# Four of seven low-part subtractions moved from POOL to DVE through a PSUM bank, weight rows of a new set requested closer together, and every fourth row's low part moved to POOL

## The chip, the core and the metric

The kernel runs on one core of one Trainium2 chip. The metric is the device time of one execution, in microseconds (us). Five engines work side by side, each on its own instruction stream, in the order in which the program gives the instructions to it: PE (TensorE, matrix products), DVE (VectorE), ACT (ScalarE), POOL (GpSimd) and SP (SyncE, which here issues nearly all DMA transfers). An instruction that waits for another engine holds up everything behind it on its own engine. A second view of PE, PEld, is the loading of weights, which overlaps the products.

## What is computed

One encoder block on x of 1024 tokens by 2048: a root-mean-square norm, one input projection, two head groups (windowed attention with a relative bias, and retention run in both directions), a norm and a gate for each branch, one output projection with a residual, and a final norm. The part that matters here is the end:

```python
mixed = jnp.concatenate([attn.astype(x.dtype), ret], axis=-1)
x = x + jnp.einsum('bse,ed->bsd', mixed, w_out[l])
return rmsnorm(x, final_norm_w)
```

Here `mixed` is 1024 by 2048 and `w_out` 2048 by 2048, both float32.

## The kernel before

**High and low parts.** PE multiplies in a rounded 32-bit format (`F32R`). To keep float32 accuracy each operand is split into a high part (the value rounded, written by ACT) and a low part (the value minus its high part). A product is then three matmuls: high by high, high by low, low by high. These are lines 1167, 1168 and 1169 in `multiply`. The stationary operand is `wh` (high) and `wl` (low); the moving one is a row, a tile `h` of 128 by 1024 whose first half is the high part and whose second half is the low part.

**Seven products.** Half of the input projection (the first pass of the loop over `slots`) and the whole output projection (the loop over `oslots`, line 1596) use a scheme with seven products, p = 0 to 6, in place of eight. In the output projection the stationary side comes from `mixed` (tile `xm`, four quarters `raws[q, 0..3]` and their combinations `sums[q]`), the moving side from combinations of `w_out`, precomputed earlier in the kernel and stored in `wc`. A tile q has seven slots, one for each p, and a slot is 12 matmuls of 512 columns: four blocks j by three. There are 16 output tiles, numbered o = q - NF from 0 to 15, so 112 slots. In `slot_list` (line 1230) the tiles interleave: (q,0), (q,1), (q-1,6), (q,2), (q-1,5), (q,3), (q,4). In the text slots of the output projection are numbered from 0, in that order.

**Rows and sets.** Four tiles o share one set of 28 rows (seven p by four j): set st = o // 4. `place` (line 1155) gives the row's buffer: it is the same for every set, `(16, 20, 0, 4, 8, 24, 12)[p] + j`, so its number modulo 4 is j. A new row therefore can't be loaded before the last matmul of the old one. After slot (q, p) of the last tile of a set (`o % 4 == 3`, line 1613) `o_rows` puts the four rows of that p for the next set into the list `todo`, from two points later on. The rows of the first set are put there while the input projection's last units run (line 1546). Stretches in which rows are replaced are called set changes: they begin in slots 19, 47 and 75, and the first slots that need the new rows are 26, 54 and 82.

**Points.** `point()` is called once per four-matmul-block step, that is once for each j: four points to a slot. Each point calls `rows_tick` (line 1045). It takes at most one row off `todo`, issues its load on SP (`row_load`), and moves the time of the next one on by `rgap` points. Ten points later the row's high part follows on ACT (`row_high`), and two points after that the low part (`row_low`, line 1040), on DVE, in place. `rows_done` (line 1061) is called ahead of a slot and forces whatever of its rows has not been given out yet. By counting points through lines 1045 to 1069 one gets the slot in which each of these instructions stands in the program. With `rgap` 2.0 the four rows of (next set, p = 4), needed in slot 32, have their loads in slots 28.25 to 29.75 and their low parts in 31.25, 31.75, 32 and 32, the last two forced by `rows_done`.

**Preparing the stationary side.** In slot n, at j = 1, `between` calls `prep` (line 1148) for slot n + 2: ACT writes `wh`, then POOL writes `wl` as source minus `wh` (`split`, line 171, with engine `G`). There are three buffers of each. `prep_sums` (line 1135) makes the combinations on POOL: four operations a tile. `raw_load` fetches the quarters on SP. So POOL does seven low parts and four combinations for each tile.

**Collecting.** After each slot DVE adds the PSUM bank to a tile (`o_collect`, line 1457). Banks are used again by later products of the same tile: slot p = 4 adds on top of the bank that p = 2 left, so its first matmul has to wait for that collect. In the last two sets ACT then squares the sums, writing the unused squares to a PSUM bank (line 1474), and in the last set `finish` (line 1480) norms a block: a short chain of small DVE operations with one POOL power in it, and four larger DVE products.

**Other work in the stretch.** The retention of the last head pairs runs through the first 18 or so slots of the output projection, with its own matmuls, its transposes into the three PSUM buffers of tag `ST` (`pS`, `pT`, lines 153 to 157), and scans on DVE.

Of the kernel before, what the change touches and what calls it, by code (L numbers as in the profile page):

```python
# [9 lines left out]
F32 = mybir.dt.float32  # L10
F32R = mybir.dt.float32r
AF = mybir.ActivationFunctionType
ALU = mybir.AluOpType
# [20 lines left out]
NS, NF = len(STD), len(FAST)  # L34
# [5 lines left out]
def hybrid_block(ctx: ExitStack, tc: tile.TileContext, a: dict, out: bass.AP):  # L40
    nc = tc.nc
    ctx.enter_context(tc.manual_schedule(engines={mybir.EngineType.Pool}))
    V, A, G, T, SP = nc.vector, nc.scalar, nc.gpsimd, nc.tensor, nc.sync
# [40 lines left out]
    def new_row(r, dt=F32R):  # L84
        rows[r] = hp.tile([128, 1024], dt, tag=f"h{r}", name=nm(f"h{r}_"), bufs=1)
        return rows[r]
# [38 lines left out]
    def flush(everything=False):  # L125
        while pend and (everything or pend[0][0] <= pt[0]):
            pend.popleft()[1]()
# [10 lines left out]
    def wpair(i):  # L138
        return w_high(), w_low()
# [10 lines left out]
    def psum(tag, bufs):  # L150
        return ps.tile([128, 512], F32, tag=tag, name=nm("ps" + tag), bufs=bufs)

    def pS():
        return psum("ST", 3)
# [7 lines left out]
    def pM():  # L162
        return [psum("Ma", 2), psum("Ma", 2), psum("Mb", 2), psum("Mb", 2)]

    def tt(eng, o, x, y, op):
        eng.tensor_tensor(o, x, y, op)  # L166
# [4 lines left out]
    def split(o_hi, o_lo, x, eng=None):  # L171
        A.copy(o_hi, x)  # L172
        tt(eng or V, o_lo, x, o_hi.bitcast(F32), ALU.subtract)
# [93 lines left out]
    def drain(queue, until):  # L267
        while until not in done:
            if not queue:
                flush(True)  # L270
                if until is None or until in done:
                    return
            g, _ = queue[0]
            try:
                queue[0] = (g, next(g))
            except StopIteration:
                queue.popleft()
# [645 lines left out]
    def spare(n):  # L923
        return rows[16 + n // 2][:, 512 * (n % 2) : 512 * (n % 2) + 512]
# [49 lines left out]
    def w_combine():  # L974
        plan = []

        def load(st, j, x, n):
            SP.dma_start(x[n], w_row(st, n // 2, n % 2, j))

        def less(x, n, m):  # L980
            tt(G, x[m], x[n], x[m], ALU.subtract)

        def less_to(x, n, m):
            tt(G, x[n], x[n], x[m], ALU.subtract)

        def keep(st, p, j, x):
            SP.dma_start(wc[st, 4 * p + j], x)

        for g in range(16):
            st, j = divmod(g, 4)  # L990
            x = [spare(4 * (g % 3) + n) for n in range(4)]
            t = 25 * g
            for n in range(4):
                plan.append((t + 4 * n, load, st, j, x, n))

            plan += [
                (t + 26, less, x, 1, 0), (t + 30, less, x, 3, 1),
                (t + 34, less_to, x, 3, 0), (t + 38, less_to, x, 2, 3),
                (t + 35, keep, st, 3, j, x[0]), (t + 39, keep, st, 4, j, x[1]),
                (t + 43, keep, st, 2, j, x[3]), (t + 47, keep, st, 5, j, x[2]),  # L1000
            ]
        yield from planned(plan)
        done.add("wc")
# [27 lines left out]
    todo, parts, rgap, rnext = deque(), deque(), [2.4], [0]  # L1031
# [7 lines left out]

    def row_low(key, r, src):  # L1040
        hi, lo = rows[r][:, 0:512], rows[r][:, 512:1024]
        tt(V, lo, lo.bitcast(F32), hi.bitcast(F32), ALU.subtract)
        done.add(key)

    def rows_tick():
# [102 lines left out]
    def prep(q, p):  # L1148
        src = {0: 0, 1: 1, 3: 2, 4: 0, 5: 3}.get(p)
        src = sums[q] if src is None else raws[q, src]  # L1150
        hi, lo = wpair(q)
        split(hi, lo, src, G)
        ready_w[q, p] = (hi, lo)

    def place(q, p, j):
# [32 lines left out]
    def quarter(b):  # L1188
        return et_(("e11", "e12", "e2", "e2")[b])
# [99 lines left out]
    for u, (kind, i) in enumerate(STD):  # L1289
# [5 lines left out]
        for pos in range(NK):  # L1295
# [35 lines left out]
            for b in range(4):  # L1331
                p = plain[b]
# [28 lines left out]
    def retention(p):  # L1361
        yield ready(("qk", p), ("vr", p), "ret")
        if p == 3:
            pace[0] = 1.9
        yield from ret_job(p)
# [23 lines left out]
    for n, (q, p) in enumerate(slots):  # L1389
# [3 lines left out]
        def between():  # L1393
            if n + 2 < len(slots):
                prep(*slots[n + 2])
            run_later()
# [19 lines left out]
    def o_rows(at, st, p):  # L1416
        for j in range(4):
            todo.append((at, ("row", st, p, j), place(NF, p, j), wc[st, 4 * p + j]))
# [101 lines left out]
    for u, (kind, i) in enumerate(FAST):  # L1520
        if u == 4:
            drain(jobs, ("attn", 3))
            drain(aux, ("sum", 3))
            drain(jobs, "attn_norm")
            flush(True)
            ph_ctx.close()
            phase[0] = ph_ctx.enter_context(tc.tile_pool(name="ret", bufs=1, reuse_waits="tile"))
            done.add("ret")
            pace[0], apace[0] = 3.0, 2.2
            e = mybir.EngineType  # L1530
            ctx.enter_context(tc.manual_schedule(engines={e.PE, e.DVE, e.Activation, e.SP}))
            for g in range(4):
                jobs.append((retention(g), None))
            for hf in range(2):
                SP.dma_start(spare(22 + hf), rbd[:, 512 * hf : 512 * hf + 512])
        if u == 0:
            for r in range(16, 28):
                new_row(r, F32)
            for hf in range(2):
                SP.dma_start(spare(12 + hf), a["cos"][:, 512 * hf : 512 * hf + 512])  # L1540
                SP.dma_start(spare(14 + hf), a["sin"][:, 512 * hf : 512 * hf + 512])
            side.append((w_combine(), None))
        whole = pM()
        if u == 13:
            rgap[0] = 3.3
            for p, at in ((0, 20), (1, 40), (2, 73), (3, 81), (4, 89), (6, 97), (5, 105)):
                o_rows(pt[0] + at, 0, p)
        elif u == NF - 1:
            rgap[0] = 2.0
        if u == 0:  # L1550
            whole = [whole[0], whole[2], whole[3], whole[1]]
        tiles = []
        for w in range(4):
            wi = W_STD + 4 * u + w
            step[0] = 16 * NS + 8 * u + 2 * w
            w_load(wi + 3)
            wh, wl = wsp.pop(wi)
            if u == 0:
                rows_done([("x", r) for r in range(4 * w, 4 * w + 4)])
            for b in range(4):  # L1560
                et, hf = b // 2, b % 2
                p = whole[b]
                if kind == "ga" and (w, b) == (2, 0):
                    attention_rows(i)
                if w == 1 + b // 2:
                    tiles.append(quarter(b))
                    SP.dma_start(tiles[b], yd[u, b])
                for kk in range(2):
                    ws = slice(256 * kk + 128 * et, 256 * kk + 128 * et + 128)
                    row = 2 * (2 * w + kk) + hf  # L1570
                    hh, hl = rows[row][:, 0:512], rows[row][:, 512:1024]
                    last = (w, kk) == (3, 1)
                    T.matmul(p, wh[:, ws], hh, start=(w, kk) == (0, 0), stop=False)  # L1573
                    T.matmul(p, wh[:, ws], hl, start=False, stop=False)  # L1574
                    T.matmul(p, wl[:, ws], hh, start=False, stop=last)  # L1575
                    if last:
                        tt(V, tiles[b], p, tiles[b], ALU.add)
                    point()
                if u == NF - 1:
                    first_slots(w, b)  # L1580
                if b == 0 and wi == W_STD:
                    w_split(wi + 1)
                if b == 1:
                    w_split(wi + 2)
        if kind == "ga":
            gates.append((attention_gates(i, tiles), None))
        elif kind == "gr":
            post.append((gate_post(kind, i, tiles), None))
        elif kind == "qk":
            post.append((rope_post(i, tiles), None))  # L1590
        else:
            post.append((value_post(i, tiles), None))
# [3 lines left out]
    for n, (q, p) in enumerate(oslots):  # L1596
        slot[0] = n
        o = q - NF
        st = o // 4
        prepare(q, p, NF)  # L1600
        for x in wanted.pop(n, ()):
            o_request(*x)

        def between():
            if n + 2 < len(oslots):
                o_ready(n + 2)
                prep(*oslots[n + 2])
            run_later()

        rows_done([("row", st, p, j) for j in range(4)])  # L1610
        multiply(q, p, between)
        o_collect(q, p)
        if o % 4 == 3 and st < 3:
            rgap[0] = 2.0
            o_rows(pt[0] + 2, st + 1, p)
    run_later(True)
    drain(aux, None)
# [104 lines left out]
```

## Time and profile before

| what | value |
|---|---|
| device time, median of 3 runs | 1531.51 us (1528.52 to 1531.87) |
| device time of the profiled execution | 1533.07 us |
| span of the profiled execution, first to last instruction | 1531.3 us |
| mean granted PE clock | 0.994 |
| output projection, first to last matmul | 1156.2 to 1516.7 us |

The page counts an engine as busy while an instruction of it runs. On PE the matmuls overlap: one is shown as 0.39 us long, while the next starts about 0.23 us after it. A small stall of PE therefore shows as idle time only where it is longer than this overlap, and the time lost is better read from how many matmuls a stretch of given length holds. In the groups a line such as L166 is that of a helper (`tt`), so groups are told apart by tiles: `wl<-r,wh` is a low part of the stationary side, `h<-h` a row's low part, `r<-r,r` a combination, `e<-psMa,e` a collect.

### The profile page before, as it was taken

How to read it: one execution, taken by the hardware profiler on the slowest of the kernel's cores; microseconds unless marked ns; L12 is line 12 of the kernel's file. 1: busy time of each engine (PE TensorE's matmuls, PEld its weight loads, DVE VectorE, ACT ScalarE, POOL GpSimd, SP SyncE). 2: the span in 40 equal slices, each digit the busy share in tenths (PEclk: the TensorE clock that was granted, in tenths of full speed). 3: DMA queues.
4: the chain of work that ended last, by engine and by line, in shares of the span. 5: the costliest groups of instructions: out<-in, count | busy, mean ns of one | idle time of the engine just before them, and what ended most of it. 6: DMA issues, size and time to landing. Idle time of an engine off the chain costs nothing.

```text
span 1531.3 us, 22172 instructions
## 1 busy us (share of the span) xinstructions
PE 1463.1 (96%) x7250; PEld 1218.4 (80%) x7250; DVE 922.0 (60%) x1791; ACT 660.4 (43%) x1401; POOL 844.6 (55%) x641
## 2 busy tenths in 40 slices
PE   8999998999999999999999999999999998989985
PEld 6998886777888888888788888788887776868764
DVE  5573333864565565565424755754869868483986
ACT  5311133775676675776221232132244243354522
POOL 3232221245546655655666656566446677687863
PEclk9999999999999999999999999999999999999998
DMA  8879889986456456446888589497496586765654
GB/s 304 287 259 337 283 264 314 283 277 203 123 168 162 135 168 186 128 153 208 308 283 268 172 278 355 164 313 271 149 305 240 157 297 217 269 241 182 206 166 144
DMA packets 225072, 353.18 MB, mean 231 GB/s; under 512 B 31883, under 2 KB 86155, under 8 KB 223548
## 3 DMA queue, kind: packets, MB, share of 16 engines
q1 hardware_dynamic: 194492, 330.78, 65.5%
q10 hardware_dynamic: 30464, 20.98, 4.4%
q8 instruction: 57, 0.93, 0.2%
q14 instruction: 59, 0.48, 0.1%
HBM read 239.97 MB, written 124.29 MB: 238 GB/s over the span
## 4 chain that ended last, share of the span: by engine, by line
PE 71%; DMA 9%; DVE 7%; issue 6%; POOL 4%; ACT 2%; SPq 1%; ACTq 0%; DVEq 0%; POOLq 0%
PE psMa L1168 5%; PE psMa L1167 5%; PE psMa L1169 5%; PE psMb L1169 4%; PE psMa L1573 4%; PE psMb L1573 4%; PE psMb L1168 4%; PE psMb L1167 4%; PE psMb L1575 4%; PE psMb L1574 4%; PE psMa L1575 4%; PE psMa L1574 4%; DVE h L166 2%; DMA h<-wc 2%; PE psST L605 2%
## 5 line engine op out<-in xcount | busy, mean ns | idle before, releaser
L166 POOL TENSOR_TENSOR wl<-r,wh 128x512 fp32r<-128x512 f32 x288 | 393.2, 1369 | 400.7 <-ACT wh L172 380.1
L172 ACT CAST wh<-r 128x512 fp32r<-128x512 f32 x288 | 177.5, 619 | 304.2 <-PE psMa L1168 70.8
L1168 PE MATMUL psMa<-h,wh 128*128 128x512 f32 x512 | 201.9, 394 | 7.4 <-DVE h L166 7.2
L1167 PE MATMUL psMa<-h,wh 128*128 128x512 f32 x512 | 203.0, 397 | 4.2 <-DVE t L166 3.5
L1169 PE MATMUL psMa<-h,wl 128*128 128x512 f32 x512 | 200.9, 392 | 0.0
L166 DVE TENSOR_TENSOR h<-h 128x512 fp32r<-128x512 f32 x156 | 174.3, 1146 | 22.9 <-ACT h L1038 22.9
L166 POOL TENSOR_TENSOR r<-r,r 128x512 f32<-128x512 f32 x128 | 182.1, 1423 | 2.8
L166 POOL TENSOR_TENSOR wl<-e,wh 128x512 fp32r<-128x512 f32 x48 | 73.0, 1523 | 199.0 <-ACT wh L172 194.9
L1169 PE MATMUL psMb<-h,wl 128*128 128x512 f32 x384 | 151.4, 394 | 7.9 <-POOL wl L166 7.8
L1167 PE MATMUL psMb<-h,wh 128*128 128x512 f32 x384 | 151.9, 396 | 3.0 <-ACT e L1201 1.7
L1168 PE MATMUL psMb<-h,wh 128*128 128x512 f32 x384 | 150.8, 393 | 2.4 <-DVE h L166 2.3
L166 DVE TENSOR_TENSOR e<-psMa,e 128x512 f32<-128x512 f32 x86 | 58.8, 685 | 106.5 <-PE psMa L1575 79.5
L1168 PEld LDWEIGHTS psMa<-h,wh 128*128 128x128 f32 x512 | 96.6, 189 | 29.4 <-DVE h L166 12.8
L1167 PEld LDWEIGHTS psMa<-h,wh 128*128 128x128 f32 x512 | 96.5, 188 | 23.1 <-issue 3.7
L1169 PEld LDWEIGHTS psMa<-h,wl 128*128 128x128 f32 x512 | 96.5, 189 | 21.0 <-POOL wl L166 0.6
L1573 PE MATMUL psMa<-h,wh 128*128 128x512 f32 x256 | 104.0, 406 | 2.5 <-DVE e L166 2.5
L1573 PE MATMUL psMb<-h,wh 128*128 128x512 f32 x256 | 103.4, 404 | 0.0
L1575 PE MATMUL psMa<-h,wl 128*128 128x512 f32 x256 | 100.0, 391 | 0.0
L1038 ACT CAST h<-h 128x512 fp32r<-128x512 f32 x156 | 90.4, 616 | 22.4 <-DMA h<-cd 9.7
L1575 PE MATMUL psMb<-h,wl 128*128 128x512 f32 x256 | 100.0, 390 | 0.0
L1574 PE MATMUL psMa<-h,wh 128*128 128x512 f32 x256 | 99.8, 390 | 0.0
L1574 PE MATMUL psMb<-h,wh 128*128 128x512 f32 x256 | 99.8, 390 | 0.0
(268 smaller groups left out, 3282.8 us busy)
## 6 DMA issues: line engine op xcount, KB each, us to landing
h<-wc SPq DMA_DIRECT2D x112, 256.0 KB, 5.1
r<-in_w_fast SPq DMA_DIRECT2D x64, 256.0 KB, 3.1
r<-in_w_half SPq DMA_DIRECT2D x64, 256.0 KB, 4.7
h<-in_w_out SPq DMA_DIRECT2D x64, 256.0 KB, 5.0
e<-yd SPq DMA_DIRECT2D x64, 256.0 KB, 4.7
wc<-h SPq DMA_DIRECT2D x64, 256.0 KB, 4.5
r<-xm SPq DMA_DIRECT2D x64, 256.0 KB, 4.1
t<-in_xT SPq DMA_DIRECT2D x31, 512.0 KB, 5.9
```

The lines of the kernel that those rows point to most:

```text
L166: eng.tensor_tensor(o, x, y, op)
L172: A.copy(o_hi, x)
L605: T.transpose(p[:, c0], x[:, c0], ident)
L1038: A.copy(rows[r][:, 0:512], rows[r][:, 512:1024].bitcast(F32))
L1167: T.matmul(bank, wh[:, ws], hh, start=(j == 0 and p in (0, 1, 3)), stop=False, skip_group_check=True)
L1168: T.matmul(bank, wh[:, ws], hl, start=False, stop=False, skip_group_check=True)
L1169: T.matmul(bank, wl[:, ws], hh, start=False, stop=(j == 3), skip_group_check=True)
L1573: T.matmul(p, wh[:, ws], hh, start=(w, kk) == (0, 0), stop=False)
L1574: T.matmul(p, wh[:, ws], hl, start=False, stop=False)
L1575: T.matmul(p, wl[:, ws], hh, start=False, stop=last)
```

## The change

Four edits, all in the lines named above. `row_low` does the low part of the rows of the output projection on POOL where the buffer's number is 3 modulo 4 (j = 3, one row in four), and on DVE otherwise. `prep` treats the output projection's products p = 0, 4, 5 and 6 differently: after the high part ACT writes a second copy of it into a PSUM buffer of tag `ST`, and DVE, not POOL, subtracts that copy from the source. Products 1, 2 and 3 stay as they were. And `rgap` is 1.4 in place of 2.0 from the last unit of the input projection on, and at each set change.

```diff
     def row_low(key, r, src):
         hi, lo = rows[r][:, 0:512], rows[r][:, 512:1024]
-        tt(V, lo, lo.bitcast(F32), hi.bitcast(F32), ALU.subtract)
+        tt(G if key[0] == "row" and r % 4 == 3 else V, lo, lo.bitcast(F32), hi.bitcast(F32), ALU.subtract)
         done.add(key)
...
         hi, lo = wpair(q)
-        split(hi, lo, src, G)
+        if q >= NF and p in (0, 4, 5, 6):
+
+            c = pS()
+            A.copy(hi, src)
+            A.copy(c.bitcast(F32R), src)
+            tt(V, lo, src, c, ALU.subtract)
+        else:
+            split(hi, lo, src, G)
         ready_w[q, p] = (hi, lo)
...
         elif u == NF - 1:
-            rgap[0] = 2.0
+            rgap[0] = 1.4
...
         if o % 4 == 3 and st < 3:
-            rgap[0] = 2.0
+            rgap[0] = 1.4
             o_rows(pt[0] + 2, st + 1, p)
```

## The prediction

> **What bounds the kernel now.** I read the page's engine shares first, then the waits of PE over the output projection (1156 to 1517 us), then a table of stretches, and last the groups of one set change.
>
> ```profile
> PE 1463.1 (96%) x7250; PEld 1218.4 (80%) x7250; DVE 922.0 (60%) x1791; ACT 660.4 (43%) x1401; POOL 844.6 (55%) x641
> ```
>
> PE is busy for 96% of the span, so little can be won except where PE stalls. The edits touch only the output projection, so only its stalls count.
>
> ```profile
> engine line waited for: us in total, times, longest us
> PE psMa L1168 <- DVE h L166: 7.2, 10, 0.7
> PE psMb L1169 <- POOL wl L166: 6.6, 5, 1.6
> PE psMa L1167 <- DVE t L166: 3.5, 3, 2.0
> PE psO L812 <- DVE ST L169: 3.2, 1, 3.2
> ```
>
> In order: the low part of a new row comes late from DVE; `wl` comes late from POOL; a bank's collect comes late from DVE; a retention scan comes late. These figures are idle time behind overlapping matmuls and understate the loss. Stretches of equal length show it whole:
>
> ```profile
> core 0: us, PE busy (x) PEld busy (x) DVE busy (x) ACT busy (x) POOL busy (x), PEclk, DMA share, GB/s
> 1256.00:1280.00 24.00, 19.73 (x79) 13.69 (x78) 23.18 (x21) 10.53 (x20) 20.28 (x13) 1.00 0.86 294
> 1290.00:1314.00 24.00, 24.00 (x108) 19.87 (x106) 8.00 (x13) 5.61 (x9) 16.87 (x14) 1.00 0.62 183
> 1339.00:1363.00 24.00, 19.76 (x81) 14.47 (x80) 23.18 (x22) 13.37 (x26) 22.96 (x15) 1.00 0.90 321
> 1364.00:1408.00 44.00, 44.00 (x196) 36.44 (x195) 18.18 (x25) 18.75 (x40) 33.01 (x25) 1.00 0.38 128
> 1420.00:1444.00 24.00, 21.12 (x87) 15.40 (x86) 23.18 (x24) 14.69 (x32) 18.90 (x13) 1.00 0.71 242
> 1456.00:1500.00 44.00, 36.85 (x154) 27.97 (x153) 34.58 (x53) 13.16 (x29) 30.98 (x26) 1.00 0.53 168
> 1156.00:1180.00 24.00, 20.80 (x111) 17.53 (x110) 23.17 (x42) 11.09 (x22) 12.46 (x12) 0.94 0.73 262
> 1180.00:1204.00 24.00, 24.00 (x132) 20.11 (x131) 21.65 (x48) 7.59 (x15) 17.05 (x12) 0.99 0.37 113
> ```
>
> A quiet 24 us holds 108 matmuls, 0.222 us each. The three set changes hold 79, 81 and 87, so they lose 29 x 0.222 = 6.4, 27 x 0.222 = 6.0 and 21 x 0.222 = 4.7 us: **17.1 us in all**. The last stretch holds 154 where a quiet 44 us holds 196: 42 x 44 / 196 = **9.4 us**. In the set changes DVE is busy 23.18 of 24 us, and in the quiet rows a third of the time. A slot takes 12 x 0.222 = 2.7 us.
>
> Why DVE is full in a set change is in its groups, here from 1245 to 1279, with POOL's beside them, and POOL's in a quiet stretch (1284 to 1322) last:
>
> ```profile
> L166 DVE TENSOR_TENSOR h<-h 128x512 fp32r<-128x512 f32 x20 | 27.7, 1421 | 0.0
> L166 DVE TENSOR_TENSOR e<-psMa,e 128x512 f32<-128x512 f32 x6 | 4.1, 680 | 2.0 <-DMA h<-wc 2.0
> L166 DVE TENSOR_TENSOR e<-psMb,e 128x512 f32<-128x512 f32 x4 | 2.7, 678 | 0.0
> ...
> L166 POOL TENSOR_TENSOR wl<-r,wh 128x512 fp32r<-128x512 f32 x10 | 15.9, 1596 | 5.6 <-ACT wh L172 5.6
> L166 POOL TENSOR_TENSOR r<-r,r 128x512 f32<-128x512 f32 x7 | 11.9, 1704 | 0.2
> ...
> L166 POOL TENSOR_TENSOR wl<-r,wh 128x512 fp32r<-128x512 f32 x15 | 20.0, 1336 | 10.2 <-ACT wh L172 10.2
> ```
>
> Three rows from DVE's order of time, the first where POOL did not overlap, the others of one operation on one value per partition:
>
> ```profile
> 1151.20 0.69 DVE L166 TENSOR_TENSOR h<-h 128x512 fp32r<-128x512 f32 x1
> ...
> 1479.48 1.24 DVE L166 TENSOR_TENSOR ft<-fv,fy 128x1 f32<-128x1 f32 x1 [1.39 <-POOL fy L166]
> 1480.76 0.16 DVE L166 TENSOR_TENSOR ft<-ft,fy 128x1 f32<-128x1 f32 x1
> ```
>
> A row's low part takes 0.69 us alone and 1.42 in the set change; POOL's subtraction takes 1.34 and 1.60. The collect, which reads one operand from PSUM, keeps its 0.68. So DVE with two SBUF operands and POOL take turns, and DVE with a PSUM operand does not. Adding turns up for the 34 us: 17 POOL operations x 1.34 + 20 rows x 0.69 = 22.8 + 13.8 = 36.6 us, about the whole stretch. Adding up DVE alone: 27.7 + 4.1 + 2.7 = 34.5. Both are full; PE waits for what they can't do.
>
> The Trainium skill, page "SBUF — State Buffer", section "SBUF: two separate sides", describes such a lock: DVE with two SBUF inputs and GpSimd share one port pair, and whichever starts first keeps it for its whole instruction. The trace agrees (1.24 against 0.16 us for the same small operation). By it, a low part read from PSUM is free of the lock; without it the sum below would keep the price of 1.42 a row, its lower bound.
>
> **The change part by part.** *Low parts of p = 0, 4, 5, 6.* Of the ten `wl` subtractions in that stretch, six leave POOL: 6 x 1.34 = 8.0 us of its turns. Each becomes a DVE subtraction with a PSUM operand; nearest row, the collect: 6 x 0.68 = 4.1 us on DVE, without a turn. ACT gets a second copy for each. ACT writing PSUM is shown by the squares, SBUF to SBUF by the high parts:
>
> ```profile
> L172 ACT CAST wh<-r 128x512 fp32r<-128x512 f32 x75 | 46.2, 620 | 89.3 <-PE psMa L1168 33.8 <-PE psMb L1168 16.8 <-DMA r<-xm 16.4
> L1038 ACT CAST h<-h 128x512 fp32r<-128x512 f32 x58 | 32.7, 615 | 0.0
> L1474 ACT ACTIVATE psO<-y 128x512 f32<-128x512 f32 x16 | 9.6, 603 | 13.5 <-DVE y L166 13.5
> ```
>
> I take 0.62 us: 16 tiles x 4 = 64 copies, 39.7 us spread over 360, hidden by ACT's idle time (10.5 to 14.7 of 24 us busy in the set changes). If that cover is gone, the high parts of rows queued behind come up to 0.62 later each. The new waits: DVE waits for ACT's copy, and the collects and rows behind it wait too. ACT can write only when slot n - 1 has freed `wh`, and DVE then has that slot's collect to do (0.68) and a row, against two ACT operations (1.24). So I cost the wait at nothing, at most 0.6 a slot where no row stands between.
>
> *Rows on POOL.* Up to the last row of p = 4, five of 20 rows leave DVE. DVE: 15 x 1.42 + 10 x 0.68 + 4.1 = 32.2 us against 34.5, if a row stays as dear: 2.3 us won. By turns: (17 - 6 + 5) x 1.34 + 15 x 0.69 = 21.4 + 10.4 = 31.8 against 36.6: **4.8 us won**. If rows fell to 0.69 DVE would need 21.3 and nothing would be late. I take the turns, since they explain the 34 us of before; the ends are 2.3 a change (6.9 in all) and the whole stall (17.1).
>
> The Trainium skill, page "GPSIMD Engine Reference", section "8. Key points", speaks against this edit: elementwise work is about twice as fast on DVE. The rows agree (1.34 against 0.69), and by them the five rows add 5 x 0.65 = 3.3 us of turns; alone they would lengthen the change to 39.9, and it is the six low parts that pay for it.
>
> *Requests at 1.4.* With 2.0 points a row, p = 4's low parts stand in the program in slots 31.25 to 32, its deadline being slot 32. With 1.4 I count 29.75 to 30.75; those of p = 3 move from 29.25-30.75 to 28.5-29.5 (due 31), those of p = 2 from 27.25-28.75 to 26.5-27.5 (due 29). That gives DVE and ACT at least one slot of slack where they had none, and without it freed time on DVE could not be used: the work stood too late in its queue. The loads go on SP's queue ahead of other loads:
>
> ```profile
> h<-wc SPq DMA_DIRECT2D x112, 256.0 KB, 5.1
> ...
> 1263.23 0.38 SPq L1035 DMA_DIRECT2D h<-wc  x1
> ...
> 1243.00:1259.00 16.00, 15.97 (x71) 12.94 (x70) 13.97 (x14) 8.78 (x17) 11.46 (x8) 1.00 1.04 367
> 1323.00:1340.00 17.00, 17.00 (x76) 14.08 (x76) 12.08 (x14) 8.16 (x16) 9.29 (x8) 1.00 1.02 385
> ```
>
> The last row of p = 4 went out at 1263.2 and took some 5 us, and DVE's rows waited for nothing (idle 0.0 in their group): loads were not what was late. But the DMA engines are full (367 to 385 GB/s) in the first third of a change, so earlier requests partly only queue. What is late next are the quarters `r<-xm` behind them; I give back 0.7 us a change for this.
>
> Set changes: 4.8 + 4.8 + 4.7 (no more was lost) - 3 x 0.7 = **12.2 us**.
>
> *Start.* From 1156 to 1204 DVE is busy 44.8 of 48 us with retention and rows. It gets about ten low parts (6.8 us), loses the j = 3 rows and some turns, and the copies now share the `ST` buffers with the retention. I take 0, between -3 (the 3.2 us wait for a scan, doubled) and +3 (gone).
>
> *End.* Counted by matmuls, three of the five late `wl` are of p = 6, two of them in the last stretch; they stood on POOL behind combinations, and now don't. Against it, DVE is behind there:
>
> ```profile
> 1463.70 0.39 PE L1167 MATMUL psMa<-h,wh 128*128 128x512 f32 x1
> ...
> 1471.82 0.68 DVE L166 TENSOR_TENSOR e<-psMa,e 128x512 f32<-128x512 f32 x1
> ```
>
> PE leaves slot 95 at 1463.7, and DVE collects it at 1471.8, 8.1 us later. A low part for slot n + 2 stands behind the collect of slot n - 1, so it comes in time only while that lag is below two slots, 5.4 us. With fewer rows left over and fewer turns I expect a smaller lag: a gain of 2 us, between +6 and -6.
>
> **Sum.** 12.2 + 0 + 2 = 14.2 us off. The profiled execution took 1533.07 us, 1.56 over the median of 1531.51: 1518.9 there, **1517.3 against the median**. Bounds: 6.9 - 3 - 6 = -2.1 and 17.1 + 3 + 6 = 26.1 us.
>
> **The rivals.** *Requests outrun the DMA engines.* At 367 to 385 GB/s nothing lands sooner; only the slack of program order and part of the turns are won. For: these two rates. Against: DVE's rows waited for no load. About 5 us won: 1526.5. *The stall moves.* Rows j = 3 stand on POOL behind combinations that wait for `r<-xm`; PE then waits for POOL's row in place of DVE's, and the sum is nothing: 1531. For: POOL is busy 18.9 to 23.0 of 24 us in the changes. Against: six operations leave for five that come, on the cheaper side. *DVE's lag decides (slower).* Where DVE is more than 5.4 us behind, each moved low part makes PE wait, and that stall delays the next. At the start and in the last stretch some ten moved low parts stand behind such lags; a loss of 1.5 us for six of them is 9, and if DVE's waits for ACT (0.6 a slot) eat the 4.8 us, nothing is won in the changes: 1531.5 + 9 = 1540.5. For: the 8.1 us. Against: a lag in a change is bounded by the work that now leaves.
>
> **Chances.** Forecast 0.65 (1510 to 1523), DMA 0.17, moved stall 0.08, DVE's lag 0.10. A measurement here can tell about 0.2%, 3 us. Faster by more than that: 0.65 + 0.17 = 0.82; same 0.08; slower 0.10. The range reaches from most of the upper bound (1508) to the DMA rival's upper side (1529); the slower case and the moved stall stay outside.
>
> **What would show it.** Right: the three 24 us stretches of a change hold some 100 matmuls or more; `h<-h` on DVE drops from 1.42 towards 1.0 us; the new subtraction takes about 0.68 whatever POOL does; waits of line 1168 for DVE's rows all but vanish. Wrong: a line 1169 waiting for DVE's `wl` by over a microsecond, a line 1168 waiting for POOL's `h`, ACT's `wh` waiting longer for `r<-xm`, or retention matmuls waiting for an `ST` buffer.

## The result, and the profile after

The changed kernel took **1518.1 us** (median of 4 runs, 1517.59 to 1521.51) against 1531.36 us for the kernel before beside it (4 runs, 1528.52 to 1531.87). The ratio is 0.9922, with a 95% interval of 0.9903 to 0.9941. The profiled execution took 1517.67 us with a span of 1515.9 us, 15.4 us less than the one of before; by the medians 13.3 us came off. In the new file the three matmul lines of `multiply` are L1174, L1175 and L1176, ACT's copy into PSUM is L1156, and `wh` of the four moved products is L1155.

Engine shares of the change, from the page:

```profile
PE 1461.7 (96%) x7250; PEld 1220.7 (81%) x7250; DVE 911.5 (60%) x1827; ACT 689.6 (45%) x1465; POOL 790.5 (52%) x605
```

The 64 moved low parts stand on DVE, whose busy time nevertheless fell by 10.5 us. POOL lost 54 us and ACT gained 29. So other work on DVE became cheaper; the groups further down show which.

What PE waited for in the change, 1156 to 1517 us (line, engine it waited for, total us, times, longest):

```profile
engine line waited for: us in total, times, longest us
PE psO L812 <- DVE ST L169: 3.1, 1, 3.1
PE psMb L1176 <- POOL wl L166: 1.9, 3, 0.7
PE psMa L1176 <- DVE wl L166: 1.9, 3, 0.9
PE psMb L1176 <- DVE wl L166: 1.0, 3, 0.4
...
PE psMb L1174 <- ACT wh L172: 0.2, 1, 0.2
...
PE psMa L1175 <- DVE h L166: 0.2, 1, 0.2
```

DVE's rows held PE for 9.5 us before (7.2 in the group that the prediction shows, 2.3 in the `psMb` one) and hold it for 0.2 now. POOL's `wl` fell from 6.6 to 1.9 in its main group, with 0.5 in another. The new wait is for DVE's own `wl`, 2.9 us in six pieces under a microsecond; five of them stand in or just behind a set change, in slots 32, 35, 37, 63 and 88. The retention's scan (L812) is where it was, and ACT's high parts, behind which the copies now stand, held PE for 0.2 us.

Stretches of the change, moved earlier so that each meets about the same slots as its counterpart of before (the columns are those of the prediction's table):

```profile
core 0: us, PE busy (x) PEld busy (x) DVE busy (x) ACT busy (x) POOL busy (x), PEclk, DMA share, GB/s
1253.00:1277.00 24.00, 22.91 (x99) 17.94 (x98) 23.04 (x25) 16.92 (x33) 21.32 (x15) 1.00 0.93 316
...
1333.00:1357.00 24.00, 22.60 (x98) 17.70 (x97) 20.69 (x24) 16.71 (x32) 19.78 (x14) 1.00 0.95 343
...
1412.00:1436.00 24.00, 23.02 (x99) 17.89 (x97) 21.11 (x26) 18.51 (x39) 17.37 (x13) 1.00 0.79 267
1440.00:1484.00 44.00, 41.55 (x177) 32.40 (x177) 38.48 (x67) 19.94 (x44) 26.39 (x22) 1.00 0.50 163
```

The set changes hold 99, 98 and 99 matmuls where they held 79, 81 and 87; 108 is a quiet stretch. What is lost behind these windows they don't show. The last stretch holds 177 where it held 154. DVE is still busy 20.7 to 23.0 of 24 us in the changes: it was relieved, not emptied.

The same by whole slots, for the kernels that the experiments use. The loss of a stretch is the distance between the first matmuls of the slots at its two ends, less 2.72 us for each slot between. The last column is the start of the output projection, which differs by 1 to 3 us between executions of one kernel (the change 1156.4 and 1159.1). Each row is one execution, and the kernel before has only one.

| us lost in | slots 19-39 | 47-67 | 75-95 | 96-111 | starts at |
|---|---|---|---|---|---|
| before | 6.6 | 6.0 | 7.0 | 9.4 | 1156.2 |
| **the change** | 3.6 | 3.1 | 3.0 | 4.6 | 1156.4 |
| the change again | 2.6 | 4.3 | 3.0 | 4.7 | 1159.1 |
| requests alone | 3.7 | 5.7 | 4.9 | 8.2 | 1154.1 |
| PSUM low parts alone | 2.0 | 5.2 | 3.3 | 6.7 | 1157.2 |
| rows on POOL alone | 6.6 | 8.1 | 10.2 | 6.8 | 1159.5 |
| requests and PSUM | 2.2 | 3.6 | 0.0 | 4.4 | 1155.3 |
| the same again | 1.5 | 4.5 | 0.0 | 4.6 | 1156.6 |
| PSUM and rows, requests at 2.0 | 1.5 | 2.5 | 1.8 | 6.6 | 1156.6 |

In the retention's part (slots 0 to 18) the change took 77.5 us against 78.4.

### The profile page after: what moved, and what is told of

Its sections match the earlier page's. It is cut to its first block, busy times and chain, and to the rows that moved or that the text cites. A ratio compares the mean times of both kernels' runs of the same rounds, so it can differ in the third digit from the quotient of the medians.

```text
span 1515.9 us, 22190 instructions
## 1 busy us (share of the span) xinstructions
PE 1461.7 (96%) x7250; PEld 1220.7 (81%) x7250; DVE 911.5 (60%) x1827; ACT 689.6 (45%) x1465; POOL 790.5 (52%) x605
## 4 chain that ended last, share of the span: by engine, by line
PE 73%; DVE 8%; DMA 6%; issue 4%; POOL 4%; ACT 3%; SPq 1%; DVEq 0%; ACTq 0%; POOLq 0%
PE psMa L1174 5%; PE psMa L1176 5%; PE psMa L1175 5%; PE psMb L1176 4%; PE psMb L1174 4%; PE psMb L1175 4%; PE psMa L1580 4%; PE psMb L1580 4%; PE psMb L1581 4%; PE psMa L1582 4%; PE psMb L1582 4%; PE psMa L1581 4%; PE psST L605 2%; DVE h L166 2%; PE psST L1353 1%
## 5 line engine op out<-in xcount | busy, mean ns | idle before, releaser
L166 POOL TENSOR_TENSOR wl<-r,wh 128x512 fp32r<-128x512 f32 x224 | 300.7, 1344 | 403.2 <-ACT wh L172 373.9
L172 ACT CAST wh<-r 128x512 fp32r<-128x512 f32 x224 | 138.4, 619 | 231.2 <-PE psMb L1581 71.2
L1174 PE MATMUL psMa<-h,wh 128*128 128x512 f32 x512 | 202.9, 396 | 2.3 <-DVE y L166 0.8
L1176 PE MATMUL psMa<-h,wl 128*128 128x512 f32 x512 | 200.9, 392 | 2.6 <-DVE wl L166 1.9
L1175 PE MATMUL psMa<-h,wh 128*128 128x512 f32 x512 | 200.4, 391 | 0.2 <-DVE h L166 0.2
L1176 PE MATMUL psMb<-h,wl 128*128 128x512 f32 x384 | 150.9, 393 | 3.4 <-POOL wl L166 2.3
L1174 PE MATMUL psMb<-h,wh 128*128 128x512 f32 x384 | 151.8, 395 | 2.2 <-ACT e L1208 1.4
L1175 PE MATMUL psMb<-h,wh 128*128 128x512 f32 x384 | 149.9, 390 | 0.0
L166 DVE TENSOR_TENSOR h<-h 128x512 fp32r<-128x512 f32 x128 | 135.0, 1081 | 18.9 <-ACT h L1038 18.7
L1176 PEld LDWEIGHTS psMa<-h,wl 128*128 128x128 f32 x512 | 96.3, 188 | 26.2 <-DVE wl L166 3.2
L1174 PEld LDWEIGHTS psMa<-h,wh 128*128 128x128 f32 x512 | 96.5, 189 | 21.3 <-ACT h L1038 3.6
L1175 PEld LDWEIGHTS psMa<-h,wh 128*128 128x128 f32 x512 | 96.5, 189 | 17.6 <-DVE h L166 0.6
```

Source lines behind the costliest of these rows:

```text
L1174: T.matmul(bank, wh[:, ws], hh, start=(j == 0 and p in (0, 1, 3)), stop=False, skip_group_check=True)
L1175: T.matmul(bank, wh[:, ws], hl, start=False, stop=False, skip_group_check=True)
L1176: T.matmul(bank, wl[:, ws], hh, start=False, stop=(j == 3), skip_group_check=True)
```

## The experiments

The theory under test is the prediction's: DVE operations with two SBUF operands and POOL's operations take turns, so a row on DVE gets dearer with what POOL does beside it. Times are medians, ratios are against the kernel before on the same chip, with 95% intervals. Each set of runs shared one chip: the kernel before took 1533.96 us beside the first four, 1531.86 beside the next four, 1531.28 beside the last four.

### Each edit alone, and two together

**Requests alone.** Both `rgap` lines.

```diff
-            rgap[0] = 2.0
+            rgap[0] = 1.4
```

> Only the requests at 1.4 points. Turns theory (the prediction's: a set change lasts as long as POOL's and DVE's SBUF operations take one after the other): turns are the same, so at most 1 us a change, 1528 to 1531. List theory (rival: DVE alone bounds a change, each row costs it about 1.4 us as long as POOL has anything to do at all): DVE's list is the same, 1530 to 1532. Order theory (third: the late place of the rows in the program was the main loss): 5 us or more won, 1526 or less.

1529.79 us, ratio 0.9971 (0.9958 to 0.9984): a gain of 4.2 us, between the 3 that turns allowed and the 5 of the order theory. The first line of PE's waits in this kernel:

```profile
PE psMb L1169 <- POOL wl L166: 12.1, 9, 2.0
```

No wait of line 1168 for DVE's rows is in that view any more, and POOL's `wl` is late by 12.1 us in place of 6.6. The requests do give slack to the rows, and the stall then largely moves to the engine beside them.

**PSUM low parts alone.**

```diff
-        split(hi, lo, src, G)
+        if q >= NF and p in (0, 4, 5, 6):
+            c = pS()
+            A.copy(hi, src)
+            A.copy(c.bitcast(F32R), src)
+            tt(V, lo, src, c, ALU.subtract)
+        else:
+            split(hi, lo, src, G)
```

> Only the four low parts through PSUM. Turns: six POOL operations fewer a change, 8.0 us of turns, so most of the 17.1 us of the changes goes, and the last stretch wins 5 to 7: about 1513. List: DVE's list grows by 6 x 0.68 = 4.1 us a change, the changes lose up to 12 us, the last stretch wins 7: 1531 to 1536, with h<-h still at 1.35 to 1.42 us.

1521.57 us, ratio 0.9924 (0.9905 to 0.9943): 12.4 us won, as much as the whole change. The list theory is out (a slower kernel), but turns had promised 1513, so they over-counted too. Rows and low parts on DVE in this kernel, 1245 to 1279 us (count, then busy us, mean ns of one, and idle before):

```profile
L166 DVE TENSOR_TENSOR h<-h 128x512 fp32r<-128x512 f32 x23 | 22.6, 1000 | 0.0
...
L166 DVE TENSOR_TENSOR wl<-r,psST 128x512 fp32r<-128x512 f32 x7 | 4.7, 678 | 0.3 <-ACT psST L1156 0.3
```

Nothing was done to the rows here, and a row fell from 1421 to 1000 ns, where the list theory had 1350 or more. The gain came without the closer requests, so the prediction's sentence that without them "freed time on DVE could not be used" does not hold.

**Rows on POOL alone.**

```diff
-        tt(V, lo, lo.bitcast(F32), hi.bitcast(F32), ALU.subtract)
+        tt(G if key[0] == "row" and r % 4 == 3 else V, lo, lo.bitcast(F32), hi.bitcast(F32), ALU.subtract)
```

> Only every fourth row's low part on POOL. Turns: 5 x 0.65 = 3.3 us more a change, about 1541. List: 5 x 1.42 = 7.1 us less on DVE a change, as far as program order lets it count: 10 to 15 us won, about 1519, and nothing won in the last stretch (1456 to 1517 of before).

1540.77 us, ratio 1.0054 (1.0035 to 1.0073): 6.8 us **slower**. Its longest wait of PE:

```profile
PE psMb L1168 <- POOL h L166: 12.2, 6, 3.7
```

PE waits for a row that now stands on POOL behind combinations and `wl`. This is the prediction's "stall moves", with a worse price than nothing. The 1541 of turns came true, but not as turns had it: DVE's rows did not get dearer (1358 ns), what PE waits for is POOL's queue.

**Requests and PSUM, all rows on DVE.** The diff of the change without its `row_low` line.

```diff
-        tt(G if key[0] == "row" and r % 4 == 3 else V, lo, lo.bitcast(F32), hi.bitcast(F32), ALU.subtract)
+        tt(V, lo, lo.bitcast(F32), hi.bitcast(F32), ALU.subtract)
```

> The change without the rows on POOL (low parts through PSUM and requests at 1.4). Turns: 8.0 us less a change and time to use it: 1508 to 1513, faster than the change. List: 4.1 us more on DVE a change, slower than the change by 10 us or more: 1528 to 1534.

1513.47 us, ratio 0.9875 (0.9856 to 0.9895). DVE's rows in this kernel, 1245 to 1279 us:

```profile
L166 DVE TENSOR_TENSOR h<-h 128x512 fp32r<-128x512 f32 x25 | 21.8, 913 | 0.0
```

DVE does 25 rows here in less time than the change's 18 (23.6 us): at these requests, rows given to POOL make those left on DVE dearer. The second execution of each kernel shows it in the price of a row (904 ns against 1192) and no longer in the sum (22.4 us for 26 rows, 19.6 for 17).

### What the PSUM operand is worth, and how far it goes

**The same subtraction from SBUF.** Requests and PSUM, but without the copy: DVE subtracts `hi` itself.

```diff
-            c = pS()
             A.copy(hi, src)
-            A.copy(c.bitcast(F32R), src)
-            tt(V, lo, src, c, ALU.subtract)
+            tt(V, lo, src, hi.bitcast(F32), ALU.subtract)
```

> As the run without the rows on POOL (low parts of p = 0, 4, 5, 6 on DVE, requests at 1.4), but DVE subtracts the high part from SBUF, and ACT's second copy and the PSUM buffer are gone. Turns theory: the moved subtraction takes turns with POOL again, its mean goes from 0.68 to 1.0 us or more, and each change gets 6 x 0.69 = 4.1 us of turns back: 1518 to 1526. Rival (only POOL's load counts, the operand doesn't matter): 1513, or a little less since ACT has 40 us less to do.

1522.73 us, ratio 0.9937 (0.9920 to 0.9955), where the PSUM operand had 0.9875: the copy, an extra operation on ACT each time, saves about 9 us (0.0062 of 1531.86; the two ratios are from two chips, and their intervals are apart). The moved low part, 1245 to 1279 us:

```profile
L166 DVE TENSOR_TENSOR wl<-r,wh 128x512 fp32r<-128x512 f32 x6 | 6.6, 1102 | 1.6 <-ACT wh L1153 1.6
```

1102 ns against 680 with the operand in PSUM, same engine, shape and place.

**All seven products through PSUM**, with requests at 1.4 and all rows on DVE, so that no low part is left on POOL.

```diff
-        if q >= NF and p in (0, 4, 5, 6):
+        if q >= NF:
```

> As the run without the rows on POOL, but all seven low parts go through PSUM, so that POOL does the four combinations of a tile alone. Turns: four POOL operations fewer in 34 us, 5.4 us of turns: the 5.8 us still lost in the three changes mostly go, 1506 to 1510, with h<-h at 0.7 to 0.8 us. Lag theory (rival: what is still lost comes from low parts that stand behind DVE's late collects): DVE gets 4 x 0.68 us more a change and more low parts behind it, 1513 to 1520, with more waits of line 1176 for DVE's wl.

1521.63 us, ratio 0.9925 (0.9909 to 0.9941). DVE's rows in this kernel, 1245 to 1279 us:

```profile
L166 DVE TENSOR_TENSOR h<-h 128x512 fp32r<-128x512 f32 x23 | 16.3, 752 | 0.0
```

Turns had promised 1506 to 1510, the lag theory 1513 to 1520: a miss for the first, and somewhat slower than even the second. The longest of PE's waits, 1156 to 1517 us:

```profile
PE psMb L1176 <- DVE wl L166: 8.3, 8, 2.2
```

With 7 POOL operations left in those 34 us a row costs 752 ns, near the 690 of a lone one, and the first change loses only 0.3 us. But every `wl` now stands in DVE's queue: slots 0 to 18 take 80.3 us against 77.1, the last 16 slots lose 8.4. The prediction's slower rival, DVE's lag, is real from here on.

**Odd rows' low part through PSUM too** (requests and PSUM, and for every odd row a second ACT copy of its high part).

```diff
+        if key[0] == "row" and r % 2:
+            rcopy[key] = pS()
+            A.copy(rcopy[key].bitcast(F32R), rows[r][:, 512:1024].bitcast(F32))
...
-        tt(V, lo, lo.bitcast(F32), hi.bitcast(F32), ALU.subtract)
+        c = rcopy.pop(key, None)
+        tt(V, lo, lo.bitcast(F32), hi.bitcast(F32) if c is None else c, ALU.subtract)
```

> As the run without the rows on POOL, but every second row's low part reads its high part from a PSUM copy that ACT writes. Turns: ten rows of 20 take no turn, 6.9 us less a change, and nothing is lost in the changes: 1507 to 1510. Rival (ACT has no room: it gets 10 x 0.58 us more in 34 us, and its waits for r<-xm hold the copies up): no better than 1513, with DVE waiting for ACT.

1515.24 us, ratio 0.9884 (0.9865 to 0.9904). Such a row took 675 ns, and the first change lost nothing. The whole was no better than without (0.9875): 1.7 us more went in slots 0 to 18 and 1.0 us more at the end. The gain expected was a miss: cheaper rows no longer decide. What does decide here no run separates.

**PSUM low parts in the last set alone.**

```diff
-        if q >= NF and p in (0, 4, 5, 6):
+        if q >= NF + 12 and p in (0, 4, 5, 6):
```

> The kernel before with the four low parts through PSUM in the last four tiles alone (o = 12 to 15), requests at 2.0 and all rows on DVE. If the gain of the last stretch (9.4 to 4.6 us lost) comes from POOL's relief there: 5 to 8 us won, the third change included, 1524 to 1527, and the first two changes lose 6.6 and 6.0 as before. If it comes from less being left over of the third change: 0 to 3 us, 1529 to 1532.

This is added to the kernel before, with nothing else. 1528.04 us, ratio 0.9971 (0.9957 to 0.9985): 3.8 us, between the two expectations. Slots 75 to 111 lost 11.1 us against 16.4, so the edit earns at the end of the kernel too, where the prediction gave it little; slots 96 to 111 alone lost 6.7 against 9.4. The first two changes, in which this kernel alters nothing, lost 5.2 and 5.2 where before lost 6.6 and 6.0: so far do single executions differ.

**All seven in the middle sets only** (o = 4 to 11), where neither the retention nor the final norm fills DVE.

```diff
-        if q >= NF and p in (0, 4, 5, 6):
+        if q >= NF and (p in (0, 4, 5, 6) or 4 <= q - NF < 12):
```

> No rows on POOL, requests at 1.4, all seven low parts through PSUM in tiles o = 4 to 11 and four of them in the first and last four tiles, where all seven made PE wait for DVE's wl. Turns and lag together: the first two changes as with all seven (0.3 and 4.6 us lost) or better, the third and the last stretch as with four (0.0 and 4.4): 1 to 3 us faster than four everywhere, 1510 to 1512. Rival (the second change is bound by loads and the first is small): the same as four everywhere within 1 us.

1515.08 us, ratio 0.9883 (0.9859 to 0.9907): the same as with four products within the intervals, a miss. A row fell to 758 ns and again nothing came of it.

### The pairs repeated on one chip

**Requests and PSUM again** (no edit against the kernel of that name above):

> The change without the rows on POOL, once more, on the same chip as the change itself: turns theory 4 to 9 us faster than the change, 1510 to 1515. If the difference of the first time was between chips: the same as the change.

1512.36 us, ratio 0.9870 (0.9848 to 0.9891). **The change again** (no edit):

> The change itself, for the comparison on one chip: ratio to the kernel before 0.990 to 0.994, about 1518 to 1520.

1520.25 us, ratio 0.9919 (0.9901 to 0.9937). The intervals are apart: with the requests at 1.4 the rows on POOL cost 7.9 us, and the kernel without them beats the change both times. In the slots of the three changes that is 3.9 us (9.7 and 9.9 lost against 5.8 and 6.0); where the rest goes the traces don't show. The four stretches of requests and PSUM, second execution, to be set beside those of the change above:

```profile
1253.00:1277.00 24.00, 23.47 (x101) 18.48 (x100) 22.02 (x30) 16.81 (x32) 14.30 (x9) 1.00 0.92 315
1333.00:1357.00 24.00, 21.32 (x90) 16.51 (x90) 20.89 (x25) 16.67 (x32) 15.09 (x10) 1.00 0.90 306
1412.00:1436.00 24.00, 24.00 (x108) 19.87 (x107) 23.53 (x31) 18.06 (x39) 14.70 (x10) 1.00 0.76 261
1440.00:1484.00 44.00, 42.00 (x182) 33.49 (x181) 36.23 (x67) 19.45 (x43) 24.52 (x21) 1.00 0.55 180
```

POOL is busy 14 to 15 of 24 us in place of 17 to 21, and the third change is as full as a quiet stretch (108). The second keeps a loss (90), and its cause stays open: in this kernel it lies in slots 54 to 64, where ACT's `wh`, a collect and POOL's `wl` are late one after the other, and no run separates them.

**PSUM and rows, requests left at 2.0.** The change with both lines taken back:

```diff
-            rgap[0] = 1.4
+            rgap[0] = 2.0
```

> The change with requests at 2.0 (low parts through PSUM and rows on POOL stay). With requests alone worth 4 us and worth 8 beside the low parts, the slack of program order counts more where turns are free. Turns theory: turns are few here, so 4 to 6 us slower than the change, 1522 to 1526. Rival (the requests only matter with no rows on POOL): within 2 us of the change.

1517.23 us, ratio 0.9906 (0.9886 to 0.9925): not slower than the change, against what turns were expected to say. The closer requests are worth 8.1 us without the rows on POOL (0.9924 to 0.9875 on one chip) and nothing that can be told with them.

The same four kernels read the other way say that the rows on POOL are not bad in themselves. With requests at 1.4 they cost 7.9 us. With requests at 2.0 and the PSUM low parts they cost nothing that can be told (0.9924 without them, 0.9906 with them, on two chips, the intervals overlapping), and in the slots of the three changes the kernel with them even lost less: 5.8 us against 10.5, one execution each. That is as little as requests and PSUM lose, though there a row cost 904 to 913 ns and here, 1245 to 1279 us:

```profile
L166 DVE TENSOR_TENSOR h<-h 128x512 fp32r<-128x512 f32 x19 | 23.1, 1237 | 0.0
```

At 2.0 the PSUM kernel's rows are what PE waits for (slots 32, 60 and 88), and moving some of them away helps; at 1.4 they are in time already. That this is the reason is an argument from the waits; no run isolates it.

## Why the prediction came out as it did

The forecast was 14.2 us off the profiled execution; 15.4 came. Against the median it was 1517.3 us, and 1518.1 came. **The total was right, two of its terms were not, and their errors cancelled: that it came so close is luck.** By whole slots, where the wait ahead of slot 95 (2.2 us lost before, nothing after) counts to the end as in the prediction, and the start is the 0.9 us of slots 0 to 18 less a start 0.2 later:

| term | predicted | measured |
|---|---|---|
| three set changes | 12.2 | 3.0 + 2.9 + 1.8 = 7.7 |
| start | 0 | about 0.7 |
| end, from slot 95 | 2 | 4.8 + 2.2 = 7.0 |

The second execution of the change gives 7.5 for the set changes and 6.9 for the end. The prediction's own 24 us windows would give (20 + 17 + 12) x 0.222 = 10.9 us for the changes, but the change loses another 3.5 us just behind them, in slots 35, 37, 63, 64, 91 and 92.

**Set changes: the term over-sized.** The step that failed is "By turns: (17 - 6 + 5) x 1.34 + 15 x 0.69". DVE's and POOL's groups of the change, 1245 to 1279 us:

```profile
L166 DVE TENSOR_TENSOR h<-h 128x512 fp32r<-128x512 f32 x18 | 23.6, 1351 | 0.0
L166 DVE TENSOR_TENSOR wl<-r,psST 128x512 fp32r<-128x512 f32 x6 | 4.1, 677 | 1.2 <-ACT psST L1156 1.2
...
L166 POOL TENSOR_TENSOR r<-r,r 128x512 f32<-128x512 f32 x7 | 11.1, 1589 | 0.2
L166 POOL TENSOR_TENSOR h<-h 128x512 fp32r<-128x512 f32 x6 | 9.6, 1614 | 3.0 <-ACT h L1038 3.0
L166 POOL TENSOR_TENSOR wl<-r,wh 128x512 fp32r<-128x512 f32 x5 | 7.4, 1480 | 5.3 <-DMA yo<-e 3.2 <-ACT wh L172 2.1
```

The sum had 16 POOL operations and 15 rows on DVE for the stretch, 31.8 us. There were 18 and 18: 18 x 1.34 + 18 x 0.69 = 36.5, as full as before (36.6). It kept 20 rows for the 34 us, but the same change issues rows closer together and PE advances faster, and 24 rows came. So a row fell only from 1421 to 1351 ns, not "towards 1.0", and the stretches ended at 98 or 99 matmuls, just short of the 100 named as the sign. In the second execution there were 17 and 17 in the same 34 us and a row took 1192 ns, so one execution tells this price to some 160 ns.

A term is missing beside it. Under "So I cost the wait at nothing" the prediction counted DVE's wait for ACT's copy, and rightly at little: 19.6 us in all for 63 low parts, 0.3 each. It gave no price to a moved low part that stands behind rows in DVE's queue in a set change. From DVE's and ACT's order of time in the change:

```profile
1274.33 4.88 DVE L166 TENSOR_TENSOR h<-h 128x512 fp32r<-128x512 f32 x3
...
1279.73 0.67 DVE L166 TENSOR_TENSOR wl<-r,psST 128x512 fp32r<-128x512 f32 x1
...
1274.57 0.58 ACT L1156 CAST psST<-r 128x512 fp32r<-128x512 f32 x1
```

ACT's copy was ready at 1275.2. DVE came to it 4.6 us later, after three rows of 1.6 us and a collect, and PE, then in slot 35, waited for it until 1280.45. It is the same in slot 37. Requests and PSUM, where a row costs 0.9 us, has neither wait.

The price of a row against POOL's work in those 34 us, from the same view of each kernel:

| kernel | POOL operations | rows on DVE | mean of a row, ns |
|---|---|---|---|
| before | 17 | 20 | 1421 |
| rows on POOL alone | 21 | 14 | 1358 |
| the change, and again | 18, 17 | 18, 17 | 1351, 1192 |
| PSUM and rows | 18 | 19 | 1237 |
| requests alone | 18 | 25 | 1201 |
| PSUM alone | 13 | 23 | 1000 |
| requests and PSUM, and again | 10, 10 | 25, 26 | 913, 904 |
| all seven, all seven in the middle sets | 7, 9 | 23, 21 | 752, 758 |

The direction of the theory holds: with 17 or more operations on POOL a row costs 1.2 to 1.4 us, with ten 0.9, with seven to nine 0.75. The arithmetic is only a guide: for requests alone it gives 18 x 1.34 + 25 x 0.69 = 41.4 us in 34, so part of the work does overlap. Nor does the price of a row give the kernel's time: turns missed the time of PSUM alone, all seven, odd rows, the middle sets, and PSUM and rows.

**The PSUM operand: right.** The new subtraction took 677 ns in the change, and 677 to 682 on the mean in this stretch of the other kernels that have it (a row's subtraction from PSUM 675), with 7 POOL operations beside it or 18; 680 was the estimate. Taken one by one over the whole change, 31 of them that a POOL operation overlapped for over 0.3 us took 680 ns on the mean, 690 at most, and 32 that none overlapped 683. With two SBUF operands it is otherwise: over the whole of the kernel before, 50 rows that no POOL operation overlapped took 684 ns (666 to 694), the other 106 took 1364. (The row at 1151.20 that the prediction calls free was not: a combination on POOL starts at 1151.42, within it, and takes 1.63 us. Its 0.69 us is the right price all the same, by these 50.) The Trainium skill, page "SBUF — State Buffer", section "SBUF: two separate sides", ties the lock to DVE instructions with two SBUF inputs; the same subtraction at 1102 and 680 ns agrees.

**Rows on POOL: the direction of the marginal cost was seen, and not acted on.** The prediction put their cost at 3.3 us of turns a change and let the moved low parts "pay for it". Measured, they cost 6.8 us alone and 7.9 us in the change; in the slots of the changes that is 1.8 us for each of three alone (24.9 lost against 19.6) and 1.3 in the change. What it did not draw from this is that the change would be faster without them. What it could not see is that they cost nothing where the requests stay at 2.0.

**Requests: half right.** That they give slack was right (the waits for DVE's rows vanish even alone). That nothing could be won without them was wrong: PSUM alone won 12.4 us. In the change itself they earn nothing that can be told; without the rows on POOL they earn 8.1 us. The 2.1 us given back for later quarters did not come either: ACT's `wh` waited 21.9 us for `r<-xm` in place of 23.7, from 1156 to 1517 us.

**Start: right.** The low parts and the copies in the shared `ST` buffers neither helped nor hurt there by more than a microsecond in the change; the one long wait, for the retention's scan, stayed at 3.1 us (3.2 before). A retention matmul did wait for an `ST` buffer that DVE had yet to read, which the prediction named as a sign of being wrong: 0.4 us in the change, 2.4 with PSUM alone and 2.2 in PSUM and rows. It cost no time there, since slots 0 to 18 still took less (77.8 and 77.5 us) than before.

**End: the term under-sized**, "a gain of 2 us, between +6 and -6". Four groups of DVE's and ACT's work in the kernel before, 1462 to 1517 us:

```profile
L169 DVE SCALAR_TENSOR_TENSOR y<-y,fy,fw 128x512 f32<-128x512 f32 x10 | 11.1, 1135 | 0.2
L166 DVE TENSOR_TENSOR ft<-fv,fy 128x1 f32<-128x1 f32 x5 | 5.1, 1022 | 2.5 <-POOL fy L166 2.4
...
L166 DVE TENSOR_TENSOR ft<-ft,fy 128x1 f32<-128x1 f32 x5 | 1.9, 383 | 0.2
...
L1474 ACT ACTIVATE psO<-e 128x512 f32<-128x512 f32 x5 | 3.0, 602 | 17.5 <-DVE e L166 17.5
```

The same groups in the change, 1447 to 1502 us, with the moved low parts:

```profile
L169 DVE SCALAR_TENSOR_TENSOR y<-y,fy,fw 128x512 f32<-128x512 f32 x12 | 10.7, 910 | 0.2
L166 DVE TENSOR_TENSOR wl<-r,psST 128x512 fp32r<-128x512 f32 x11 | 7.5, 678 | 0.4 <-ACT psST L1156 0.4
...
L166 DVE TENSOR_TENSOR ft<-fv,fy 128x1 f32<-128x1 f32 x7 | 4.3, 619 | 3.8 <-POOL fy L166 3.7
...
L166 DVE TENSOR_TENSOR ft<-ft,fy 128x1 f32<-128x1 f32 x6 | 1.0, 160 | 0.2
...
L1481 ACT ACTIVATE psO<-e 128x512 f32<-128x512 f32 x5 | 3.0, 601 | 9.4 <-DVE e L166 9.4
```

DVE took on 11 subtractions (7.5 us), and its other work with two SBUF operands became cheaper: the products of `finish` 910 ns in place of 1135, the one-value operations 619 and 160 in place of 1022 and 383. On ACT the squares, behind which the next `wh` stands, waited 9.4 us for DVE's sums in place of 17.5. The prediction named "fewer rows left over and fewer turns" and gave them 2 us without a sum; it had the row from which the turns could be priced (1.24 against 0.16 us) and used it for the set changes only.

Both causes show. In slots 96 to 111 three kernels with PSUM low parts and requests at 2.0 lost 6.6 to 6.7 us (PSUM alone, the last set alone, PSUM and rows), where before lost 9.4; with requests at 1.4 the change and the kernel without rows on POOL lost 4.4 to 4.7 in two executions each. So of the 4.8 us some 2.7 go with the PSUM low parts and 2 with the requests: in slot 98 PE waits for a moved low part for 1.7 and 2.0 us in PSUM alone and PSUM and rows, and for 0.4 in the change. How exact this is: executions of one kernel differ by 0.1 to 0.2 us here, but the kernel before has one, and rows alone, which alters no instruction of these slots, lost 6.8.

**The rivals.** The DMA rival is not what limited: rows on DVE came in time, and requests paid 8.1 us where POOL had room. The moved stall did not come in the change, but it did with rows alone, and for 2.6 us in PSUM and rows. DVE's lag did not make the kernel slower with four products, but it is part of what the set changes still lose: its marks, waits for DVE's `wl`, are 2.9 us in the change and 8.3 us with seven.

## What to carry to other kernels

Where DVE and POOL both work on SBUF, count POOL's operations in the stretch as a cost on DVE's, and look first for an operand that can be read from PSUM: here that was worth 9 us, though ACT had to write a copy for it. Count work per slot and not per microsecond when an edit also makes the stretch run faster or its requests denser. Time each part of a bundled change alone, left out, and in pairs: this one was carried by the PSUM operand. Beside it either the closer requests or the rows on POOL did no harm, the requests won 8 us, and both together lost those 8 us again.

## What the runs showed of the hardware

- A 128x512 subtraction on DVE with two SBUF operands took from 752 to 1421 ns on the mean of a stretch, less with fewer POOL operations beside it; with one operand in PSUM 675 to 682 ns. Even operations on one value per partition went from 383 to 160 ns where POOL had 22 operations beside them in 55 us in place of 30.
- ACT wrote the 128x512 copy into PSUM in 582 ns, against 619 ns for the same copy into SBUF. These are its groups in the change, 1156 to 1502 us; 620 had been taken for both, and the 36.6 us of copies hid in ACT's idle time, as the prediction had it:

```profile
L1155 ACT CAST wh<-r 128x512 fp32r<-128x512 f32 x63 | 39.0, 619 | 44.4 <-PE psMa L1175 24.3 <-PE psMb L1175 7.1 <-DMA h<-wc 4.2
L1156 ACT CAST psST<-r 128x512 fp32r<-128x512 f32 x63 | 36.6, 582 | 0.0
```

- POOL pays in the contention too. In the kernel before a combination took 1348 ns on the mean in the quiet stretch from 1284 to 1322 us and 1704 in the first set change. In the first set change of the other kernels it took 1488 to 1719; that range is not in the order of their POOL operations.
